# A hybrid decoder layer on one core: transposes at another channel step, LoRA products of a couple's second pair in another turn

## The chip, the cores and the metric

The kernel runs on one core of one Trainium2 chip. The metric is the device time of one execution in microseconds; lower is better. Times before are three runs; one further execution was profiled.

## What is computed

A decoder layer on 2048 rows of 1024 channels in float32: RMS norm, one input projection, two kinds of recurrent heads side by side (four HGRN2 heads of 128 and eight RWKV-7 heads of 64), one output projection, then a gated feed-forward block with a causal convolution, and a last norm. The part that the change touches is the input projection and RWKV's decay and learning rate:

```python
h = _rmsnorm(x, norm1_w[l])
proj = h @ w_in[l]
...
w = -jax.nn.softplus(-(w0 + jnp.tanh(wd) @ w2)) - 0.5      # decay, low-rank ("LoRA")
decay = jnp.exp(-jnp.exp(w))
a = jax.nn.sigmoid(a0 + ad @ a2)                           # learning rate, low-rank
...
kk = heads(k * k_k)
kk = kk / jnp.maximum(jnp.sqrt(jnp.sum(kk * kk, axis=-1, keepdims=True)), L2_EPS)
k = k * (1.0 + (a - 1.0) * k_a)
y = _rwkv7_scan(heads(r), heads(decay), heads(k), heads(v), -kk, kk * heads(a))
```

## The kernel before

The kernel has two stages. The first, up to about 1260 us of the profile, makes the input projection, both kinds of heads and the output projection of the first three blocks of 512 rows; the second makes the rest. Only the first is touched.

The first stage is written as three Python generators whose steps are interleaved by hand. In each round the loop at the stage's end (from L1172 on) lets `rw_super` make one step (a *turn*), then `hg_unit` one, and then calls `fill`, which lets `dense` go on until a budget is used up: `TICK` = 2000 for most rounds, 1.5 or 0.9 times that in some. A channel step of `dense` costs 648 of it, and 436 more where a transpose was issued beside it. So the text puts about three channel steps between two turns.

- `dense` makes the projection column by column: 128 output channels by 512 rows. A column has eight channel steps (`k` = 0 to 7) of three matmuls each (`mm3`, L270 to L272, the high and low parts of the split operands), all into one accumulator in a bank `pj`. After `k` = 7 the column is evicted by ScalarE and VectorE. There are two `pj` banks: one for the column at work, the other for the previous one until it is evicted.
- Beside a column, `dense` issues transposes of rows for later: `turn` (L447, tile `xt`) transposes one 128-channel slice of the next block's normed rows, `turn2` (L457, tile `h`) one of the rows for the second norm, and stores it. Each is four transposes into a `pj` bank and one eviction on ScalarE; `turn2` also sends one store from SP. They lie in the list `turns`; a column takes one at `k` = 1 and, if the list still has one, a second at `k` = 5. There are 24 of the first kind and 16 of the second.
- `rw_super` handles a couple of head pairs: eight RWKV heads are four pairs, a couple is two pairs, so that there are two couples in each of four blocks, eight in all. `U` runs over the couple's pairs. Its matmuls write double banks with the tag `rw`, of which there are two. Its first turn multiplies the LoRA weights `w2a2` with `tl` for both pairs (L722, L723; two products for each pair, one `rw` bank for each pair) and takes the sigmoids `a` and `iW` on ScalarE; its second turn makes a running sum of `iW` on VectorE (`scan`, L731), the squares of the keys and `km` on ScalarE, and splits the squares into high and low parts (`parts`); its third takes exponentials and adds the squares up over a head by matmuls with `group` (L1140, L1141). The last turn of the couple before ends in a product `gm` in an `rw` bank (L991) that VectorE reads at L993.
- `act` loads a table set on ScalarE (L118) whenever a function needs another set than the one before it in the text; sigmoid is in one set, logarithm and exponential are in another. `hg_unit` uses the latter in one of its turns (tile `osq`).

The order of instructions on each engine is fixed when the program is built. It is near that of the text, but not the same: where an instruction's operands or its buffer are judged not to be ready, others that come later in the text go first.

Of the kernel before, what the change touches and what calls it, by code (L numbers as in the profile page):

```python
# [11 lines left out]
AF = mybir.ActivationFunctionType  # L12
ALU = mybir.AluOpType
# [54 lines left out]
def tile_layer(ctx, tc, consts, x, norm1_w, w_in, hg_lb_logits, hg_norm_w, rw_shift_mu, rw_w0, rw_w2,  # L68
# [4 lines left out]
    V, S, TE = nc.vector, nc.scalar, nc.tensor  # L73
# [23 lines left out]
    scanm = cst[:, C_SCAN:C_SCAN + 512]  # L97
# [16 lines left out]
    def act(out_, in_, func, **kw):  # L114

        want = tables.get(func)
        if want is not None and want != tab["now"]:
            pre = S.preload_act_table_set(want)  # L118
            for u_ in tab["uses"]:
                tc.add_manual_dep(pre.ins, u_.ins.name, NOSYNC, reason="table order")  # L120
            tab.update(now=want, pre=pre, uses=[])
        i_ = S.activation(out_, in_, func, **kw)  # L122
        if want is not None:
            tc.add_manual_dep(i_.ins, tab["pre"].ins.name, NOSYNC, reason="table order")
            tab["uses"].append(i_)
        return i_
# [32 lines left out]
    def vec(nm, i):  # L159
        return vt[:, off[nm] + i:off[nm] + i + 1]  # L160
# [20 lines left out]
    oka = cp.tile([P, 16], F32, name="oka")[:, 0:4]  # L181
# [76 lines left out]
    def transposed(xt, nm, psum, evict):  # L258

        n = len(xt)  # L260
        for k in range(KD):
            tp = psum()
            for i in range(n):
                TE.transpose(tp[:, i * P:(i + 1) * P], xt[i][:, k * P:(k + 1) * P], ident)
            evict(k, tp[:, :n * P], vec(nm, k))
            yield 109 * n
# [7 lines left out]
    def phase1(c1):  # L274
# [6 lines left out]
        w2a2 = hp.tile([P, 512], F32, name="w2a2")  # L281
# [156 lines left out]
        def four_tiles(t_):  # L438
            return [t_[:, i, :] for i in range(4)]
# [105 lines left out]
        def spread():  # L545

            while True:
                yield bank("hg")
                yield bank("hg")
                for _ in range(2):  # L550
                    t_ = ps.tile([P, 2, BLK], F32, tag="rw", name="rw", bufs=2)
                    yield t_[:, 0]
                    yield t_[:, 1]

        def dense():
# [49 lines left out]
            def load(i):  # L605
                if i < len(cols) and i not in loaded:
                    ws, ct = [], cols[i] // P
                    for k2 in range(2):
                        if i < NCOL:
                            raw = wp.tile([P, 4, P], F32, tag="wraw", name="wraw", bufs=4)  # L610
                            wload(raw, w_in[0, k2 * 512:k2 * 512 + 512, cols[i]:cols[i] + P].rearrange("(k p) c -> p k c", p=P))
                            ws.append(split(wp, raw, [P, 4, P], "w", 4))
                            for c in range(2):
                                nc.gpsimd.dma_start(Win[ct][k2][c], ws[k2][c].bitcast(F32))
                        else:
                            ws.append(tuple(wp.tile([P, 4, P], F32R, tag="w" + c, name="w" + c, bufs=4) for c in "hl"))
                            for c in range(2):
                                wload(ws[k2][c].bitcast(F32), Win[ct][k2][c])
                    loaded[i] = ws
# [4 lines left out]
            turns = []  # L624
            for n, jb in enumerate(jobs):
                if jb[0] == "E":
                    jb[1]()
                    continue
                if jb[0] == "A":
                    if jb[1] == 0:  # L630
                        banks = spread()
                        ahead = transposed(four_tiles(rows[0]), "n1", lambda: next(banks), to_h)
                    continue
                if jb[0] == "T":
                    turns.append(jb[1])
                    continue
                if jb[0] in "OW":
                    while done["rw2"] < 2 * jb[1] + 2 or done["hg"] < 4 * jb[1] + 4:
                        yield None
                    if jb[0] == "W":  # L640
                        jb[2]()
                    else:
                        yield from (out_block(2, *rows["O"]) if jb[1] == 2 else out_block(jb[1], then=jb[1] + 2, ahead=lambda i=i: load(i)))
                    continue
                if jb[0] == "L":
                    while done["rw1"] < 2 * jb[1] + 4 or done["rw2"] < 2 * jb[1] + 2 or done["hg"] < 4 * jb[1] + 4:
                        yield None
                    (o_half if jb[1] == 2 else o_load)(jb[1])
                    continue
                _, col, ev, cond, fin = jb  # L650
                after = jobs[n + 1][1] if jobs[n + 1][0] == "O" and jobs[n + 1][1] < 2 else None
                while not cond():
                    yield None
                load(i)
                ws = loaded.pop(i)
                if i == 0:
                    next(ahead)
                    next(ahead)
                    constants()
                if jobs[n + 1][0] != "O":  # L660
                    load(i + 1)
                i += 1
                acc = bank("pj")
                then = jobs[n + 1][1] if jobs[n + 1][0] == "A" else None
                for k in range(KD):
                    wh, wl = ws[k // 4]
                    next(ahead, None)
                    mm3(acc, (wh[:, k % 4, :], wl[:, k % 4, :]), (hh[:, k, :], hl[:, k, :]), k == 0, k == KD - 1)
                    aside = k in (1, 5) and len(turns) > 0
                    if aside:  # L670
                        turns.pop(0)()
                    if k == KD - 1:
                        ev(acc)
                        if fin is not None:
                            fin()
                    next_block(then, k)
                    if after is not None:
                        next_out(after, k)
                    yield 648 + 436 * aside
# [18 lines left out]
        U = range(2)  # L698

        def rw_super(nb, s_):  # L700

            tl = stage[("tl", nb)]
            r, k, v = (stage.pop(("rkv", nb, s_, w)) for w in range(3))
            prs = (2 * s_, 2 * s_ + 1)
            pc = [slice(p * P, (p + 1) * P) for p in prs]
# [4 lines left out]
            def bank2():  # L710
                return ps.tile([P, 2, BLK], F32, tag="rw", name="rw", bufs=2)

            def parts(src):
                hi, lo = (rp.tile([P, 2, BLK], F32R, tag=tag, name="part") for tag in ("XH", "E"))
                split_to(hi, lo, src)
                return hi, lo

            ai = tile_("KBT", [2, 2, BLK], "ai")
            a, iW = ai[:, 0], ai[:, 1]
            bs_ = [bank2() for _ in U]  # L720
            for u in U:
                TE.matmul(bs_[u][:, 0, :], w2a2[64:128, pc[u]], tl[64:128, :], start=True, stop=True)  # L722
                TE.matmul(bs_[u][:, 1, :], w2a2[0:64, pc[u]], tl[0:64, :], start=True, stop=True)  # L723
            for u in U:
                act(a[:, u], bs_[u][:, 0, :], AF.Sigmoid, bias=vec("a0", prs[u]))
                act(iW[:, u], bs_[u][:, 1, :], AF.Sigmoid, bias=vec("w0", prs[u]))
            yield
            mk_ = tile_("M", [4, 2, BLK], "mk")
            c, km, sq = mk_[:, 0], mk_[:, 1], mk_[:, 2]
            for u in U:  # L730
                V.tensor_tensor_scan(c[:, u], scanm, iW[:, u], 0.0, ALU.mult, ALU.add)  # L731
                act(sq[:, u], k[:, u], AF.Square, scale=vec("kk", prs[u]))
                act(km[:, u], a[:, u], AF.Identity, bias=oka[:, prs[u]:prs[u] + 1], scale=vec("ka", prs[u]))
            hi, lo = parts(sq)
            yield
            W = tile_("UV", [16, 65], "W")
            WC = tile_("WC", [16, 1], "WC")
# [186 lines left out]
            for u in U:  # L924
                Q, G = M[:, 0, u, :, :, 0:64], M[:, 1, u, :, :, 0:64]
                yg = bank2()
                for w in range(2):
                    for b in range(4):
                        for e in range(2):
                            rs_ = slice(er0(e), er0(e) + 64)  # L930
                            sl = w * 256 + b * 64
                            for h in range(2):
                                rhs = (M[rs_, e, u, b, h, 64:128] if w == 0
                                       else KBT[rs_, u, 2 * b + e, h * 64:h * 64 + 64])
                                TE.matmul(yg[h * 64:h * 64 + 64, e, sl:sl + 64], Q[rs_, b, h, :], rhs,
                                          start=True, stop=True, tile_position=(er0(e), h * 64))
# [8 lines left out]
            for u in U:  # L945
                for ch in range(8):
                    b, e = ch // 2, ch % 2
                    for h in range(2):
# [3 lines left out]
                                  stop=False, tile_position=(0, c0), skip_group_check=True)  # L952
            WC2 = WC.rearrange("p (u c) t -> p u c t", u=2)
            for ch in range(8):
                b, e = ch // 2, ch % 2
                cs_ = slice(ch * 64, ch * 64 + 64)
                for u in U:
                    for h in range(2):
                        hr = slice(h * 64, h * 64 + 64)
                        TE.matmul(xp[hr, u, cs_], M[hr, 1, u, b, e, 0:64], XH[hr, u, ch, :], start=False,  # L960
                                  stop=ch == 7, tile_position=(h * 64, h * 64), skip_group_check=True)
                for u in U:
                    for h in range(2):
                        hr, c0 = slice(h * 64, h * 64 + 64), (h ^ u) * 64
                        TE.matmul(yp[c0:c0 + 64, u, cs_], XH[hr, u, ch, :], RT[hr, u, ch, :], start=False,
                                  stop=ch == 7, tile_position=(h * 64, c0), skip_group_check=True)
# [234 lines left out]
    with ExitStack() as c2:  # L1201
# [36 lines left out]
        with tc.tile_pool(name="op", bufs=1, reuse_waits="tile") as op_:  # L1238
# [61 lines left out]
            for dh in range(2):  # L1300
                accs = [pst("wacc") for _ in range(4)]
                for n, k in enumerate((0, 1, 4, 5, 2, 3, 6, 7)):
# [22 lines left out]
                    for q in range(12):  # L1325
                        i, t_ = (q % 4, q // 4) if first else (q // 3, q % 3)
                        TE.matmul(accs[i], terms[t_][0][:, i * P:(i + 1) * P], terms[t_][1],
                                  start=n == 0 and t_ == 0, stop=n == KD - 1 and t_ == 2)
# [353 lines left out]
```

## Time and profile before

| | us |
|---|---|
| three runs | 2602.02, 2597.45, 2592.02; median 2597.45 |
| profiled execution | 2593.87 |
| its span, first to last instruction | 2592.1 |
| PE busy | 2526.2 (97%) |
| VectorE (DVE) busy | 1961.6 (76%) |
| ScalarE (ACT) busy | 1381.2 (53%) |
| GpSimd (POOL) busy | 371.4 (14%) |

PE is TensorE's matmuls, PEld its weight loads, which overlap them. A group's row names the line, the engine, the operation, the tiles written and read, the shape and the count, then busy time and mean length of one, then the engine's idle time before them and what ended it. In the timeline a row is start, length, engine, line, operation, tiles and count; a bracket at its end is the idle time before it and who ended it. A matmul's end is modelled: where matmuls overlap, their rate is read from the distance of the starts.

### The profile page before, as it was taken

How to read it: one execution, taken by the hardware profiler on the slowest of the kernel's cores; microseconds unless marked ns; L12 is line 12 of the kernel's file. 1: busy time of each engine (PE TensorE's matmuls, PEld its weight loads, DVE VectorE, ACT ScalarE, POOL GpSimd, SP SyncE). 2: the span in 40 equal slices, each digit the busy share in tenths (PEclk: the TensorE clock that was granted, in tenths of full speed). 3: DMA queues.
4: the chain of work that ended last, by engine and by line, in shares of the span. 5: the costliest groups of instructions: out<-in, count | busy, mean ns of one | idle time of the engine just before them, and what ended most of it. 6: DMA issues, size and time to landing. Idle time of an engine off the chain costs nothing.

```text
span 2592.1 us, 50957 instructions
## 1 busy us (share of the span) xinstructions
PE 2526.2 (97%) x19467; PEld 2034.7 (78%) x19467; DVE 1961.6 (76%) x3744; ACT 1381.2 (53%) x2266; POOL 371.4 (14%) x660
## 2 busy tenths in 40 slices
PE   7999999999999999999999999999999999999998
PEld 6777778777777777777788888877888878888887
DVE  4878777685666866788687799988988887666555
ACT  5556554564445644355567644565555454455444
POOL 6433222222222122231000000000000000000000
PEclk9999999999999999999999999999999999999999
DMA  8846455575745657676663477757653564988655
GB/s 310 240 156 192 154 161 146 156 207 176 210 156 159 196 176 196 237 222 171 234 206 126 141 258 252 231 178 232 215 196 101 180 200 134 330 313 289 195 187 191
DMA packets 379722, 518.98 MB, mean 200 GB/s; under 512 B 113887, under 2 KB 210517, under 8 KB 379477
## 3 DMA queue, kind: packets, MB, share of 16 engines
q1 hardware_dynamic: 325361, 337.38, 41.0%
q0 software_dynamic: 54048, 178.32, 21.5%
q8 instruction: 153, 2.51, 0.4%
q14 instruction: 92, 0.75, 0.1%
q10 hardware_dynamic: 68, 0.02, 0.0%
HBM read 372.99 MB, written 134.22 MB: 196 GB/s over the span
## 4 chain that ended last, share of the span: by engine, by line
PE 58%; issue 14%; DVE 12%; DMA 6%; ACT 5%; POOL 4%; SPq 0%; POOLq 0%; DVEq 0%; ACTq 0%
PE pj L270 6%; PE pj L271 5%; PE pj L272 5%; PE ua L270 4%; PE ua L272 4%; PE ua L271 4%; PE da L270 3%; PE da L271 3%; PE da L272 3%; PE db L271 2%; PE db L272 2%; PE db L270 2%; PE ud L272 2%; PE ud L270 2%; PE ud L271 2%
## 5 line engine op out<-in xcount | busy, mean ns | idle before, releaser
L270 PE MATMUL pj<-hh,wh 128*128 128x512 f32 x960 | 394.6, 411 | 1.3 <-ACT xt L122 0.9
L271 PE MATMUL pj<-hl,wh 128*128 128x512 f32 x960 | 378.3, 394 | 0.0
L272 PE MATMUL pj<-hh,wl 128*128 128x512 f32 x960 | 378.0, 394 | 0.0
L270 PE MATMUL ua<-Bh,uwh 128*128 128x512 f32 x704 | 277.0, 393 | 4.0 <-ACT m L122 3.7
L272 PE MATMUL ua<-Bh,uwl 128*128 128x512 f32 x704 | 274.5, 390 | 1.9 <-DVE uwl L255 1.9
L271 PE MATMUL ua<-Bl,uwh 128*128 128x512 f32 x704 | 274.2, 389 | 0.0
L270 PEld LDWEIGHTS pj<-hh,wh 128*128 128x128 f32 x960 | 180.9, 189 | 47.0 <-issue 4.9
L272 PEld LDWEIGHTS pj<-hh,wl 128*128 128x128 f32 x960 | 180.9, 188 | 40.4 <-issue 1.2
L271 PEld LDWEIGHTS pj<-hl,wh 128*128 128x128 f32 x960 | 181.2, 189 | 36.2 <-issue 3.2
L254 ACT CAST uwh<-uraw 128x512 fp32r<-128x512 f32 x220 | 134.5, 617 | 132.6 <-PE ua L271 53.5
L255 DVE TENSOR_TENSOR dal<-draw,dah 128x512 fp32r<-128x512 f32 x138 | 95.2, 690 | 110.9 <-ACT dah L254 110.5
L254 ACT CAST dah<-draw 128x512 fp32r<-128x512 f32 x138 | 85.8, 622 | 164.2 <-PE da L271 77.3
L255 DVE TENSOR_TENSOR uwl<-uraw,uwh 128x512 fp32r<-128x512 f32 x220 | 147.0, 684 | 34.6 <-ACT uwh L254 34.4
L270 PEld LDWEIGHTS ua<-Bh,uwh 128*128 128x128 f32 x704 | 132.1, 188 | 35.9 <-ACT m L122 8.9
L272 PEld LDWEIGHTS ua<-Bh,uwl 128*128 128x128 f32 x704 | 132.2, 188 | 30.5 <-DVE uwl L255 2.8
L271 PEld LDWEIGHTS ua<-Bl,uwh 128*128 128x128 f32 x704 | 132.2, 188 | 26.7
L270 PE MATMUL ud<-Bh,uwh 128*128 128x512 f32 x352 | 138.0, 392 | 0.0
L272 PE MATMUL ud<-Bh,uwl 128*128 128x512 f32 x352 | 137.1, 390 | 0.0
L271 PE MATMUL ud<-Bl,uwh 128*128 128x512 f32 x352 | 137.0, 389 | 0.0
L1552 POOL DMA_DIRECT2D gd<-y x2 | 1.1, 541 | 945.9 <-DVE y L1550 945.9
L271 PE MATMUL da<-dbl,dah 128*128 128x512 f32 x332 | 129.5, 390 | 0.2 <-DVE dbl L255 0.2
L272 PE MATMUL da<-dbh,dal 128*128 128x512 f32 x332 | 129.2, 389 | 0.0
(589 smaller groups left out, 6181.1 us busy)
## 6 DMA issues: line engine op xcount, KB each, us to landing
uraw<-in_w_up_dram SPq DMA_DIRECT2D x176, 256.0 KB, 3.2
br<-gd SPq DMA_DIRECT2D x88, 256.0 KB, 4.2
draw<-Sg SPq DMA_DIRECT2D x88, 256.0 KB, 2.8
draw<-Tw SPq DMA_DIRECT2D x88, 256.0 KB, 3.8
gd<-y SPq DMA_DIRECT2D x86, 256.0 KB, 2.8
Sg<-br SPq DMA_DIRECT2D x72, 256.0 KB, 2.2
xt<-x1d SPq DMA_DIRECT2D x32, 512.0 KB, 6.6
wraw<-in_w_in_dram POOLq DMA_DIRECT2D x60, 256.0 KB, 4.8
```

Of the source, the lines that this page charges most:

```text
L254: S.copy(hi, src)
L255: V.tensor_sub(lo, src, hi.bitcast(F32))
L270: TE.matmul(acc, lh, rh, start=first, stop=False, skip_group_check=skip)
L271: TE.matmul(acc, lh, rl, start=False, stop=False, skip_group_check=skip)
L272: TE.matmul(acc, ll, rh, start=False, stop=last, skip_group_check=skip)
L1552: (dma if end is None else nc.gpsimd.dma_start)(gd_[2 * h + b][fb * P:(fb + 1) * P, :], ys[0][:, b * BLK:(b + 1) * BLK])
```

## The change

Two edits in the first stage. A column's first transpose stands at channel step 2 instead of 1. In `rw_super` the LoRA products and sigmoids of the couple's second pair go from the first turn to the second, where the running sums and `km` of both pairs follow; the squares of the keys and their split go from the second turn to the first. The number of turns is the same, and no instruction is added or removed in the text.

```diff
-                    aside = k in (1, 5) and len(turns) > 0
+                    aside = k in (2, 5) and len(turns) > 0
...
-            bs_ = [bank2() for _ in U]
-            for u in U:
-                TE.matmul(bs_[u][:, 0, :], w2a2[64:128, pc[u]], tl[64:128, :], start=True, stop=True)
-                TE.matmul(bs_[u][:, 1, :], w2a2[0:64, pc[u]], tl[0:64, :], start=True, stop=True)
-            for u in U:
-                act(a[:, u], bs_[u][:, 0, :], AF.Sigmoid, bias=vec("a0", prs[u]))
-                act(iW[:, u], bs_[u][:, 1, :], AF.Sigmoid, bias=vec("w0", prs[u]))
-            yield
             mk_ = tile_("M", [4, 2, BLK], "mk")
             c, km, sq = mk_[:, 0], mk_[:, 1], mk_[:, 2]
+
+            def lora(u):
+                b_ = bank2()
+                TE.matmul(b_[:, 0, :], w2a2[64:128, pc[u]], tl[64:128, :], start=True, stop=True)
+                TE.matmul(b_[:, 1, :], w2a2[0:64, pc[u]], tl[0:64, :], start=True, stop=True)
+                act(a[:, u], b_[:, 0, :], AF.Sigmoid, bias=vec("a0", prs[u]))
+                act(iW[:, u], b_[:, 1, :], AF.Sigmoid, bias=vec("w0", prs[u]))
+
+            def scan(u):
+                V.tensor_tensor_scan(c[:, u], scanm, iW[:, u], 0.0, ALU.mult, ALU.add)
+                act(km[:, u], a[:, u], AF.Identity, bias=oka[:, prs[u]:prs[u] + 1], scale=vec("ka", prs[u]))
+
+            lora(0)
             for u in U:
-                V.tensor_tensor_scan(c[:, u], scanm, iW[:, u], 0.0, ALU.mult, ALU.add)
                 act(sq[:, u], k[:, u], AF.Square, scale=vec("kk", prs[u]))
-                act(km[:, u], a[:, u], AF.Identity, bias=oka[:, prs[u]:prs[u] + 1], scale=vec("ka", prs[u]))
             hi, lo = parts(sq)
+            yield
+            lora(1)
+            for u in U:
+                scan(u)
             yield
```

## Prediction

> **What bounds the kernel now.** I read the busy table first, then stages, then PE's groups with their idle time, then the timeline around the two edited places.
>
> ```profile
> span 2592.1 us, 50957 instructions
> PE 2526.2 (97%) x19467; PEld 2034.7 (78%) x19467; DVE 1961.6 (76%) x3744; ACT 1381.2 (53%) x2266; POOL 371.4 (14%) x660
> ...
> 50.00:1240.00 1190.00, 1156.80 (x13437) 912.10 (x13436) 869.15 (x2075) 635.29 (x1054) 322.12 (x572) 1.00 0.62 186
> 1240.00:2592.10 1352.10, 1333.82 (x5880) 1094.41 (x5878) 1068.96 (x1614) 720.32 (x1163) 16.43 (x30) 1.00 0.63 209
> ```
>
> PE is the bound: busy 97% of the span, at granted clock 1.00 in both stages. All edited code runs in the first stage. From 50 to 1240 us PE is idle 1190.0 - 1156.8 = 33.2 us, spread over 1.2 ms; no edit here removes PE work, so only a part of those 33 us can be won. The groups name the part that touches the edit:
>
> ```profile
> L270 PE MATMUL pj<-hh,wh 128*128 128x512 f32 x960 | 394.6, 411 | 1.3 <-ACT xt L122 0.9 <-DVE hq L346 0.2
> L1140 PE MATMUL rw<-part,group 128*128 128x512 f32 x48 | 19.7, 410 | 1.3 <-ACT part L247 1.3
> L1141 PE MATMUL rw<-part,group 128*128 128x512 f32 x48 | 19.3, 401 | 0.4 <-DVE part L248 0.4
> L722 PE MATMUL rw<-tl,w2a 64*128 64x512 f32 x32 | 17.4, 633 | 3.7 <-DVE yo L993 2.5 <-ACT ai L122 1.2
> L447 PE MATMUL pj<-ident,xt 128*128 128x128 f32 x96 | 15.1, 279 | 4.4 <-DVE hgg L370 2.0 <-DVE hq L346 1.4 <-ACT hf L122 0.9
> L457 PE MATMUL pj<-ident,xt 128*128 128x128 f32 x64 | 9.9, 275 | 0.7 <-ACT h L122 0.4 <-DVE hq L346 0.4
> ```
>
> These are groups of PE's instructions: busy us, mean ns of one, then the idle time before them and what ended it. The LoRA products (L722) wait 3.7 us. The transposes of the next block's rows (L447) wait 4.4 us, those of the second norm (L457) 0.7: 5.1. The head sums (L1140, L1141) wait 1.7. Everything that the edit names is 10.5 us, 0.4% of the span.
>
> **How far the order on the engines is that of the text.** A couple's timeline on PE:
>
> ```profile
> 485.69 0.69 PE L722 MATMUL rw<-tl,w2a 64*128 64x512 f32 x1
> ...
> 488.01 0.39 PE L272 MATMUL pj<-hh,wl 128*128 128x512 f32 x1
> 488.25 0.40 PE L270 MATMUL pj<-hh,wh 128*128 128x512 f32 x1
> 489.41 0.69 PE L722 MATMUL rw<-tl,w2a 64*128 64x512 f32 x1 [0.77 <-ACT ai L122]
> ...
> 490.47 0.50 PE L271 MATMUL pj<-hl,wh 128*128 128x512 f32 x1
> ...
> 492.43 0.40 PE L1140 MATMUL rw<-part,group 128*128 128x512 f32 x1
> ```
>
> The text issues a couple's four products in one go (each shows as two instructions), but on PE the second head pair's two start 3.7 us after the first, with dense matmuls between. So the builder had judged the second `rw` bank not yet free and had put ready matmuls ahead; it only guessed 0.77 us too short. Matmuls follow each other every 0.23 us (488.01 to 488.25), so a channel step of three is 0.69 us, though a single one shows 0.39. The head sums, two turns behind, come 8 dense matmuls later (490.47 to 492.43): a turn is about 9 dense matmuls, 2.1 us, and other heads' work.
>
> **Part 1, the second pair a turn later.** How many `pj` matmuls already lie between the pairs of the six couples that wait, by the table of stretches for that tile (length, then PE's busy us and its count in brackets), and below them the waits from the timeline:
>
> ```profile
> 204.79:207.90 3.11, 2.57 (x10) 1.78 (x10) 0.17 (x1) 0.60 (x1) 1.00 0.01 3
> 348.75:351.20 2.45, 2.11 (x8) 1.41 (x8) 0.00 (x0) 0.09 (x1) 1.00 0.00 0
> 486.76:489.40 2.64, 1.88 (x7) 1.22 (x7) 0.00 (x0) 0.60 (x1) 1.00 0.38 135
> 658.96:660.80 1.84, 1.17 (x5) 0.75 (x5) 0.00 (x0) 0.00 (x0) 1.00 0.86 324
> 799.55:802.20 2.65, 2.11 (x8) 1.41 (x8) 0.03 (x1) 0.60 (x1) 1.00 0.65 198
> 1121.14:1123.30 2.16, 1.08 (x4) 0.75 (x4) 0.00 (x0) 0.00 (x0) 1.00 0.55 197
> ```
>
> ```profile
> 351.28 0.69 PE L722 MATMUL rw<-tl,w2a 64*128 64x512 f32 x1 [0.42 <-ACT ai L122]
> 660.84 0.69 PE L722 MATMUL rw<-tl,w2a 64*128 64x512 f32 x1 [0.72 <-DVE yo L993]
> 802.24 0.66 PE L722 MATMUL rw<-tl,w2a 64*128 64x512 f32 x1 [0.58 <-DVE yo L993]
> 1123.35 0.69 PE L722 MATMUL rw<-tl,w2a 64*128 64x512 f32 x1 [0.58 <-DVE yo L993]
> ```
>
> A turn later means at least 9 between. The cover grows by 0, 1, 2, 4, 1 and 5 matmuls of 0.23 us. The waits are 0.42, 0.77, 0.72, 0.58 and 0.58 as quoted, and 3.7 less these, 0.6, in the first. What is left of them: 0.6, 0.19, 0.31, 0, 0.35, 0, in sum 1.45. Gain: 3.7 - 1.45 = 2.2 us. Ends: 0 (the builder puts the pair where it stands) and 3.7 (all gone). I take 2.2, because the row count says the move is only some 2 matmuls on average. Behind the waiting pair on PE stand only dense matmuls; nobody else waits for it. In the other two couples (60.87 and 981.94) the second pair never waited, so a turn's delay of 2.1 us gains nothing; it makes the second scan later there, and dense matmuls cover that, as between 485.69 and 489.41. The pair's sigmoids go along on ACT, the second `scan` and `km` follow on DVE and ACT in the turn in which they stood before. No DMA moves with this part, and neither SP's nor POOL's queue is passed.
>
> **Part 2, squares a turn sooner.** In the trace they are long done:
>
> ```profile
> 475.66 0.71 ACT L122 ACTIVATE mk<-rkv,vt 128x512 f32<-128x512 f32 x1
> ...
> 479.52 1.05 ACT L247 CAST part<-mk 128x1024 fp32r<-128x1024 f32 x1 [1.59 <-PE rw L1140]
> ```
>
> Square at 475.66, cast done at 480.57, 5.1 us before the first product at 485.69 and 12 us before the sums that read it (492.43). A turn sooner in the text changes nothing that PE sees: 0. Ends: -1.7 us (the head sums' waits, were they these sums') and +0.7 (the two squares a place too early on ACT, 0.71 ahead of an eviction).
>
> **Part 3, transposes at step 2.** A transpose at step 1 must find the bank that the previous column's accumulator held. The dense matmuls from a column's first up to its transposes, by the same kind of table, for the three longest waits, and the waits:
>
> ```profile
> 239.57:243.00 3.43, 1.51 (x7) 0.93 (x5) 0.68 (x1) 0.59 (x1) 1.00 0.88 185
> 497.89:503.00 5.11, 3.63 (x15) 2.36 (x13) 0.72 (x1) 0.60 (x1) 1.00 0.73 210
> 824.26:827.00 2.74, 1.53 (x7) 0.93 (x5) 0.70 (x1) 0.60 (x1) 1.00 0.45 124
> ```
>
> ```profile
> 243.02 0.66 PE L447 MATMUL pj<-ident,xt 128*128 128x128 f32 x4 [1.39 <-DVE hq L346]
> 503.07 0.66 PE L447 MATMUL pj<-ident,xt 128*128 128x128 f32 x4 [1.36 <-DVE hgg L370]
> 827.06 0.65 PE L447 MATMUL pj<-ident,xt 128*128 128x128 f32 x4 [0.62 <-DVE hgg L370]
> ```
>
> Of each count one is the previous column's last. So at 243.02 and 827.06 the transposes stand at 6 matmuls, where the text puts them; at 503.07 at 14, already later than step 2 (9), and the move does nothing there. Three matmuls more cover 0.69 of the 1.39 and all of the 0.62: 1.3 us gained. The smaller waits I count at nothing. Ends: 0 and 5.1. I take 1.3, by these rows. What goes along: four transposes, the eviction on ACT (`xt`, 0.60; `h`, 0.69) and, for eight of the second kind, a store on SP, 0.69 us later and past no other transfer that waits for it. What comes late next is the bank: the tile of step 2 must be out three steps, 9 x 0.23 = 2.07 us, later for a second tile at step 5, instead of four. That I cost at nothing; it is the third rival.
>
> **Sum.** 2.2 + 0 + 1.3 = 3.5 us off the span, 2592.1 to 2588.6. The profiled execution took 2593.87 us with 1.8 around the span, so 2590.4. The three runs' median, 2597.45, lies 3.6 above the profiled one; on its scale the forecast is 2594.0. That is 0.13%, under the 0.5% (13 us) that a measurement here tells from no change.
>
> **Rivals.**
>
> *It doesn't do what it says* (15%): the builder fills PE by its own guess of readiness, as the 7 matmuls ahead of 489.41 show, and ends with the same order. 2597.5. Against it: at 243.02 and 827.06 the text's place was kept.
>
> *All the named waits go* (15%): 10.5 us, 2587 on the median's scale. For it: none of the waits is over 1.4 us, about one turn. Against it: the 1.36 at 503.07 stands at 14 matmuls, where a later step in the text does not reach. A redrawn order of the whole first stage might carry it further; its entire idle time is 33.2 us, and under 2584 some 40% of that would have to go.
>
> *Slower: the second tile waits for the bank* (13%). Eight columns carry two tiles. If an eviction ends over 2.07 us after its transposes start, the next transposes stop PE, and behind them the column.
>
> ```profile
> 984.66 0.60 PE L457 MATMUL pj<-ident,xt 128*128 128x128 f32 x4
> ...
> 986.12 0.70 ACT L122 ACTIVATE h<-pj,vt 128x512 f32<-128x512 f32 x1
> ```
>
> Here it ended 2.16 us after (986.82 - 984.66), longer than the three steps that will be left. If all eight lose the whole step, 8 x 0.69 = 5.5 us; with part 1's gain and without part 3's, 2597.45 - 2.2 + 5.5 = 2600.8. It decides against the change once more than five of the eight lose a step (5 x 0.69 = 3.5).
>
> *Slower: tables* (7%). Sigmoids in two turns instead of one can have a head's logarithm and exponential between them, and each such couple needs two more table loads.
>
> ```profile
> L118 ACT ACT_TABLE_LOAD x50 | 64.2, 1283 | 0.9
> ...
> 1124.53 1.26 ACT L122 ACTIVATE ai<-rw,vt 128x512 f32<-128x512 f32 x2 [1.32 <-PE rw L723]
> 1125.81 1.28 ACT L118 ACT_TABLE_LOAD   x1
> 1127.11 0.69 ACT L122 ACTIVATE osq<-hg,eps 128x512 f32<-128x512 f32 x1
> ```
>
> For it: in the last couple a head's logarithm (1127.11) already stands right behind the sigmoids. Price: at most 16 loads of 1.283, 20.5 us of ACT, which is idle half the stage. If all of it showed, 2594.0 + 20.5 = 2614.5; if one couple has it and it shows, 2594.0 + 2.6 = 2596.6. [...]
>
> **How the numbers follow.** Part of the waits goes: 50%, 2594.0. The rivals hold 15, 15, 13 and 7%. The range reaches down past 2587 by the spread of the runs (2592.02 to 2602.02, about 5 either way) to 2581, and up past the bank's 2600.8 by some 3 to 2604; without the far ends of the last two rivals some two in ten lie outside. The likeliest case alone has 2589 to 2599. Faster by over 0.5% needs the tail of the second rival, 6%; slower by over 0.5% the full price of the tables or both slow rivals, 5%; the rest, 89%, is within.
>
> **What would show it.** L722's idle time falls from 3.7 to about 1.5 and L447's and L457's together from 5.1 to about 3.8; the second pair stands 9 or more dense matmuls behind the first; squares still end before the products; the table loads between 50 and 1262 us stay near 50; the second stage stays at its time. The prediction is wrong if the first stage's PE idle time moves by more than 10 us, which would be a redrawn order and not the named waits, or if `h` or `xt` appears as a releaser of the dense matmuls with more than today's 0.9.

## Result and the profile after

The changed kernel took 2606.3 us (median of 16 executions, 2599.3 to 2614.2) against 2597.9 for the kernel before (16, 2590.8 to 2602.9): ratio 1.0027, 95% interval 1.0016 to 1.0037. By the medians it is 8.4 us slower, some 0.3%; the forecast was 3.5 us faster, and its range ended at 2604. In two later comparisons the same kernel had 1.0031 (1.0019 to 1.0044) and 1.0020 (1.0010 to 1.0030).

The profiled execution of the changed kernel happens to be its slowest (2614.17) and that of the kernel before a quick one (2593.87). So the two profiles lie 20 us apart where the medians lie 8.4 apart: kinds and places are read from them, sizes from the timed ratios.

The busy table of the changed kernel:

```profile
span 2612.2 us, 50948 instructions
...
PE 2537.7 (97%) x19467; PEld 2044.8 (78%) x19467; DVE 1963.4 (75%) x3744; ACT 1382.9 (53%) x2266; POOL 371.0 (14%) x660
```

Its two stages by the table of stretches (length, then busy us and instructions of PE, PEld, DVE, ACT and POOL, then granted clock, DMA share, GB/s):

```profile
50.00:1240.00 1190.00, 1151.28 (x13181) 906.83 (x13183) 858.85 (x2046) 627.42 (x1039) 322.88 (x574) 0.99 0.60 183
1240.00:2612.20 1372.20, 1353.42 (x6151) 1111.97 (x6151) 1081.57 (x1643) 730.89 (x1179) 17.85 (x32) 1.00 0.63 209
```

The second stage kept its length: from its first matmul on the tile `ua` to the end it takes 1287.5 us before and 1289.2, 1286.9 and 1285.3 in the three profiles of the changed kernel (`after_again` and `after_again2` are the other two). So the loss lies in the first, where PE has done 13181 matmuls by 1240 us instead of 13437. Two things took time there: PE idles 1190.0 - 1151.3 = 38.7 us instead of 33.2, and its clock was granted at half rate for 23.9 us of the stage instead of 10.2 (added up from the clock records). The clock's column has to be read closely: a mean that reads 1.00 or 0.99 still holds 10 or 24 us at half rate.

PE's groups, those that the prediction named and those that grew (line numbers behind the edit are 3 or 7 higher than before: L722 is L725, L1140 is L1147, L960 is L967, L886 is L893; in the kernels below with a line `late` they are 3 or 11 higher):

```profile
L270 PE MATMUL pj<-hh,wh 128*128 128x512 f32 x960 | 397.9, 415 | 1.4 <-ACT xt L122 0.6 <-ACT hv L122 0.5
L270 PE MATMUL pj<-wh,hh 128*128 128x512 f32 x160 | 66.3, 420 | 8.4 <-DVE hgg L370 5.4 <-DVE xh L417 2.7
L271 PE MATMUL pj<-wl,hh 128*128 128x512 f32 x160 | 63.8, 399 | 2.2 <-DVE wl L255 2.2
L967 PE MATMUL rw<-XH,M 64*64 64x64 f32 x512 | 29.2, 231 | 1.7 <-DVE XH L974 1.7
L1147 PE MATMUL rw<-part,group 128*128 128x512 f32 x48 | 20.0, 417 | 3.6 <-ACT part L247 3.6
L725 PE MATMUL rw<-tl,w2a 64*128 64x512 f32 x32 | 18.0, 642 | 1.8 <-ACT ai L122 1.6
L447 PE MATMUL pj<-ident,xt 128*128 128x128 f32 x96 | 15.0, 280 | 0.8 <-DVE hq L346 0.8
L457 PE MATMUL pj<-ident,xt 128*128 128x128 f32 x64 | 9.8, 275 | 0.1
L893 PE MATMUL rw<-TTs,ZT 32*32 32x32 f32 x512 | 7.9, 195 | 2.9 <-ACT ZT L122 2.6
```

Before, the groups of these that the prediction did not show were:

```profile
L270 PE MATMUL pj<-wh,hh 128*128 128x512 f32 x160 | 66.1, 420 | 7.3 <-DVE hgg L370 5.4 <-DVE xh L417 1.7
L271 PE MATMUL pj<-wl,hh 128*128 128x512 f32 x160 | 64.1, 401 | 0.0
L960 PE MATMUL rw<-XH,M 64*64 64x64 f32 x512 | 29.5, 230 | 0.1
L886 PE MATMUL rw<-TTs,ZT 32*32 32x32 f32 x512 | 7.6, 194 | 1.8 <-ACT ZT L122 1.7
```

The edit did what it was read to do, and more: the LoRA products' idle time fell from 3.7 to 1.8 us, the transposes' from 5.1 to 0.9. These 6.1 us, and more, came back elsewhere: the head sums (L1147) rose from 1.3 to 3.6, the product on `XH` from 0.1 to 1.7, the output projection from 7.3 to 8.4 behind `xh` and from 0 to 2.2 behind its weights `wl`, the products on `ZT` from 1.8 to 2.9, in sum 8.3 us. The rest of the 5.5 us more is spread over groups that rose by 1 us or less each.

### The profile page after: what moved, and what is told of

It is laid out like the page before. It is cut to its first block, busy times and chain, and to the rows that moved or that the text cites. A ratio compares the mean times of both kernels' runs of the same rounds, so it can differ in the third digit from the quotient of the medians.

```text
span 2612.2 us, 50948 instructions
## 1 busy us (share of the span) xinstructions
PE 2537.7 (97%) x19467; PEld 2044.8 (78%) x19467; DVE 1963.4 (75%) x3744; ACT 1382.9 (53%) x2266; POOL 371.0 (14%) x660
## 4 chain that ended last, share of the span: by engine, by line
PE 61%; issue 13%; DVE 11%; DMA 7%; ACT 4%; POOL 3%; SPq 0%; POOLq 0%; DVEq 0%; ACTq 0%
PE pj L270 5%; PE pj L271 5%; PE pj L272 5%; PE ua L270 5%; PE ua L272 5%; PE ua L271 5%; PE da L271 3%; PE da L272 3%; PE da L270 3%; PE ud L272 2%; PE ud L270 2%; PE ud L271 2%; PE db L270 2%; PE db L272 2%; PE db L271 2%
```

## The experiments

Each ratio is against the kernel before on the same chip, with its 95% interval. The kernel before had medians of 2597.7, 2595.0, 2596.7 and 2597.2 us beside the four sets. The ratio is not the quotient of the medians and differs from it by up to 0.001.

**First set: which half of the change.** `turns_only` is the kernel before with the transposes' edit; `rw_only` with all of the edit in `rw_super` and the transposes at step 1; `squares_only` with the squares a turn sooner and both LoRA pairs in the first turn; `after_again` is the changed kernel.

```diff
turns_only, against before:
-                    aside = k in (1, 5) and len(turns) > 0
+                    aside = k in (2, 5) and len(turns) > 0
squares_only, against before:
-            yield
             mk_ = tile_("M", [4, 2, BLK], "mk")
             c, km, sq = mk_[:, 0], mk_[:, 1], mk_[:, 2]
             for u in U:
-                V.tensor_tensor_scan(c[:, u], ...)
                 act(sq[:, u], ...)
-                act(km[:, u], ...)
             hi, lo = parts(sq)
             yield
+            for u in U:
+                V.tensor_tensor_scan(c[:, u], ...)
+                act(km[:, u], ...)
+            yield
```

> Only the transposes go to step 2; the LoRA products stay in the first turn. Theory CHAIN (the loss comes from the LoRA edit, which makes a couple's chain on ACT and DVE later, so that PE waits at its head sums): 2594 to 2598, that is 0 to 4 us under before, with L447 and L457 idle under 1.5 us together. Rival BANK (a step less for the second transposes): 2602 to 2606, with xt or h as releasers of dense matmuls. Rival CLOCK (short PE stops cluster and trip half-clock windows, whichever edit causes them): the time follows the number of windows at half clock, about 1.7 us for each 3.4 us.

> Only the LoRA and squares edit; transposes stay at step 1. Theory CHAIN: 2603 to 2608, all or more of the loss, with the head sums' idle time near 4 us as in the changed kernel and BV's cast about 1.5 us later in the first couple. Rival BANK: 2594 to 2598. Rival CLOCK: in between, and more than two half-clock windows.

> Only the squares go a turn sooner; the LoRA products of both pairs stay in the first turn. Built, the order on every engine is that of the kernel before, so all theories expect no change, 2594 to 2602, and the profile is a second one of the kernel before: CHAIN and BANK expect its stops at the same places within 0.3 us; CLOCK expects that the number and place of half-clock windows may differ.

> The changed kernel once more, for a second profile on the same chip as the parts. CHAIN: 2602 to 2610, head sums idle again near 4 us. CLOCK: 2602 to 2610, and half-clock windows again more than two before 1260 us; where the first profile's windows were luck, the count falls to two or three and the profiled time with it by about 1.7 us for each.

| kernel | us | ratio to before | interval |
|---|---|---|---|
| turns_only | 2596.8 | 1.0002 | 0.9988 to 1.0016 |
| rw_only | 2600.6 | 1.0020 | 1.0011 to 1.0029 |
| squares_only | 2595.4 | 0.9997 | 0.9985 to 1.0008 |
| after_again | 2603.7 | 1.0031 | 1.0019 to 1.0044 |

The squares do nothing that these runs can tell. The transposes alone neither gain nor lose, so the bank of the second tile costs nothing by itself; they keep 3.2 us of their waits, where CHAIN expected under 1.5. The LoRA edit alone loses. By the medians it loses less than the whole change (2600.6 against 2603.7) and less than the 2603 that CHAIN expected at least, though the two intervals overlap. Against CLOCK: the profile of `turns_only` has 20.5 us at half clock in the first stage, as `after_again` has, and took 2593.5 us, as long as that of the kernel before with 10.2. So the time at half clock alone does not give the loss.

**Second set: which couples.** In these the second pair is a turn later only in some of the eight couples, numbered 0 to 7 (squares as in the changed kernel; where the pair is not later, its products follow the first pair's sigmoids in the text):

```diff
+            late = 2 * nb + s_ in (1, 2, 3, 4, 5)
             lora(0)
+            if not late:
+                lora(1)
             for u in U:
...
             yield
-            lora(1)
+            if late:
+                lora(1)
             for u in U:
                 scan(u)
```

`lora_1to5` has the couples 1 to 5 as shown, `lora_06` has 0 and 6, `lora_7` the last, all with the transposes at step 1; `lora_1to5_turns` is `lora_1to5` with the transposes at step 2.

> Second pair a turn later in the last couple alone; transposes at step 1. Theory TABLES IN THE LAST COUPLE (its second sigmoids stand behind a head's logarithm, exponential and two table loads; the second scan is 3 us later; a half-clock window follows near 1208 us): 2600 to 2603, the whole loss of rw_only. Rival NO-WAIT COUPLES (the loss comes from the first and seventh couples, where the second pair never waited): 2596 to 2598. Rival SCATTER (no couple carries it): 2597 to 2600.

> Second pair a turn later in the first and the seventh couple alone, where it never waited before; transposes at step 1. TABLES IN THE LAST COUPLE: 2596 to 2598. NO-WAIT COUPLES: 2600 to 2603, with the first couple's BV cast 1.5 us later and more idle time at the head sums and at the products behind them. SCATTER: 2597 to 2600.

> Second pair a turn later in the second to sixth couples, where it waited 3.1 us in all before; transposes at step 1. TABLES IN THE LAST COUPLE and NO-WAIT COUPLES: 2595 to 2597.5, some 1 to 2 us of the LoRA waits gone and nothing lost. SCATTER: 2598 to 2600.

> As lora_1to5, with the transposes at step 2. If the two edits do not touch each other: 2594 to 2597, below the kernel before. If they do (the transposes' stop in the fourth couple is gone and PE comes 1.8 us early to the head sums, then waits at XH and xh and meets half-clock windows near 510, 588 and 773 us as in the changed kernel): 2599 to 2602.

| kernel | us | ratio to before | interval |
|---|---|---|---|
| lora_7 | 2597.0 | 1.0011 | 1.0000 to 1.0021 |
| lora_06 | 2595.2 | 0.9999 | 0.9991 to 1.0008 |
| lora_1to5 | 2595.7 | 1.0001 | 0.9993 to 1.0010 |
| lora_1to5_turns | 2599.1 | 1.0020 | 1.0009 to 1.0032 |

Two places lose: the last couple by itself, and something in the couples 1 to 5 that neither edit makes alone (1.0002 and 1.0001) but both together do. The first is only just seen in the times: the interval of `lora_7` begins at 1.0000, and its 2597.0 us lie under the 2600 to 2603 that were expected. The traces show it more clearly.

*The last couple.* ACT's timeline in the changed kernel:

```profile
1135.71 1.27 ACT L122 ACTIVATE ai<-rw,vt 128x512 f32<-128x512 f32 x2 [0.53 <-PE rw L726]
1136.99 1.28 ACT L118 ACT_TABLE_LOAD   x1
1138.29 0.69 ACT L122 ACTIVATE osq<-hg,eps 128x512 f32<-128x512 f32 x1
...
1139.58 0.62 ACT L122 ACTIVATE osq<-osq 128x512 f32<-128x512 f32 x1
1140.22 1.28 ACT L118 ACT_TABLE_LOAD   x1
1141.51 1.26 ACT L122 ACTIVATE ai<-rw,vt 128x512 f32<-128x512 f32 x2
```

Before, the second pair's sigmoids (1124.53) followed the first pair's by 3.3 us:

```profile
1121.24 1.27 ACT L122 ACTIVATE ai<-rw,vt 128x512 f32<-128x512 f32 x2 [0.53 <-PE rw L723]
```

Now it is 5.8: the head's logarithm and exponential, with a load on either side, have moved between the pairs. How long a couple takes is read from its first LoRA product to its last product `gm` (both by their lines' list of instructions, count, shortest/median/longest, first and last start), here for the last couple before and after:

```profile
L722 PE MATMUL rw<-tl,w2a x4: 589/641/694, 1120.1 to 1123.9; 64*128 64x512 f32 x4
L991 PE MATMUL rw<-gdt,g x8: 590/592/630, 1116.2 to 1247.9; 128*128 128x512 f32 x8
```

```profile
L725 PE MATMUL rw<-tl,w2a x4: 589/642/694, 1134.5 to 1138.4; 64*128 64x512 f32 x4
L998 PE MATMUL rw<-gdt,g x8: 590/592/647, 1130.6 to 1265.9; 128*128 128x512 f32 x8
```

127.8 us (1247.9 - 1120.1) has become 131.4. Over all 18 profiled executions of this case, read in the same way, the last couple takes 130.5 to 131.9 us in the seven where its second pair is later and 127.4 to 128.6 in the eleven where it is not.

*The clock.* The table of stretches, for the changed kernel, cut so that each pair is the 3.41 us before a stretch at half clock and that stretch:

```profile
506.99:510.40 3.41, 1.64 (x8) 0.94 (x7) 3.41 (x5) 2.48 (x4) 0.73 (x2) 0.99 0.87 315
510.40:513.81 3.41, 3.41 (x11) 2.79 (x10) 3.21 (x4) 0.60 (x1) 0.00 (x0) 0.51 0.65 223
...
1216.89:1220.30 3.41, 2.13 (x80) 1.33 (x76) 3.32 (x10) 3.05 (x7) 0.00 (x0) 1.00 0.49 175
1220.30:1227.13 6.83, 6.72 (x69) 5.33 (x70) 6.18 (x17) 2.79 (x7) 2.15 (x4) 0.50 0.51 155
```

PE was idle for 52% and 38% of the stretch before, and the next ran at 0.5. With the last couple's pair later PE comes to `ZT` and `TTs` ahead of ACT, some 85 us behind the couple's start: in `lora_7` PE is idle there for 53% of 3.41 us, and the half clock follows.

```profile
1203.49:1206.90 3.41, 1.60 (x67) 1.05 (x66) 3.35 (x10) 3.12 (x8) 0.54 (x1) 0.99 0.36 125
1206.90:1210.31 3.41, 3.41 (x51) 2.84 (x53) 3.41 (x9) 0.81 (x3) 1.61 (x3) 0.51 0.57 192
```

A half-clock stretch that starts between 1206 and 1221 us is in all seven profiles with the last couple's pair later and in none of the eleven others. In the changed kernel dense matmuls start 0.42 us apart inside a half-clock stretch (511.31 to 511.73) and 0.23 outside (514.06 to 514.29), so a stretch costs at most about half its length, here 1.7 or 3.4 us; this is an estimate.

**Third set: where the two edits meet.** In the traces of `turns_only` and `lora_1to5_turns` the fourth couple (3) starts at nearly the same time, its first LoRA product at 489.62 and 489.28 us. The fifth starts at 662.27 and 666.71, so the fourth takes 172.7 us in one and 177.4 in the other, 4.8 more. Its stop near 507 us, in `turns_only`, then in `lora_1to5_turns`:

```profile
506.89 0.33 PE L447 MATMUL pj<-ident,xt 128*128 128x128 f32 x1 [1.28 <-DVE hgg L370]
```

```profile
506.60 0.50 PE L1151 MATMUL rw<-part,group 128*128 128x512 f32 x1 [1.77 <-ACT part L247]
...
624.81 0.39 PE L971 MATMUL rw<-XH,M 64*64 64x64 f32 x6 [2.58 <-DVE XH L978]
```

The stop at the transposes is gone, but the head sums stop at the same time. Behind it PE comes to the product on `XH` 2.6 us before VectorE has made it; a stretch of 3.41 us at half clock follows at 625.5 (1.7 us lost, by the same estimate). 2.6 + 1.7 = 4.3 is most of the 4.8. What VectorE is doing, in the changed kernel, with ACT's rows that it waits for:

```profile
622.19 0.07 DVE L745 MEMSET W<- 128x16 f32 x1
627.01 0.75 DVE L435 TENSOR_SCALAR xt<-xt,nst 128x1024 f32<-128x1024 f32 x1 [4.75 <-ACT nst L122]
627.68 0.28 DVE L974 TENSOR_TENSOR XH<-rw,WC 128x128 f32<-128x128 f32 x1
```

```profile
616.51 1.06 ACT L122 ACTIVATE nsq<-xt 128x1024 bf16<-128x1024 f32 x1 [6.01 <-DMA xt<-x1d]
...
623.43 1.06 ACT L122 ACTIVATE nsq<-xt 128x1024 bf16<-128x1024 f32 x1 [1.27 <-DMA xt<-x1d]
...
625.11 1.28 ACT L118 ACT_TABLE_LOAD   x1
```

`XH` stands on VectorE behind the norm (L435) of the first block's rows, which come back from DRAM (`x1d`) for the second norm. That waits 4.75 us for ACT's factors, these for a table load, that for the last square, and that for a transfer. A chain that has nothing to do with the couple holds its `XH`. In the kernel before, `XH` stands behind the same norm, but PE has no wait for it there:

```profile
615.51 0.75 DVE L435 TENSOR_SCALAR xt<-xt,nst 128x1024 f32<-128x1024 f32 x1 [2.67 <-ACT nst L122]
616.18 0.28 DVE L967 TENSOR_TENSOR XH<-rw,WC 128x128 f32<-128x128 f32 x1
```

Four kernels test the place:

```diff
c3_turns, not3_turns, after_no7: as in the second set, transposes at step 2, with
+            late = 2 * nb + s_ in (3,)
+            late = 2 * nb + s_ in (1, 2, 4, 5)
+            late = 2 * nb + s_ in (0, 1, 2, 3, 4, 5, 6)
after_n_later, against the changed kernel:
-                              (at[nb] + 7, ("E", norm4(("N", nb - 2))))]
-                    extra += [(at[nb] + 8 + k // 2, ("T", turn2(...
+                              (at[nb] + 7 + 2 * (nb == 2), ("E", norm4(("N", nb - 2))))]
+                    extra += [(at[nb] + 8 + 2 * (nb == 2) + k // 2, ("T", turn2(...
```

> The second pair later in the fourth couple alone, transposes at steps 2 and 5. FOURTH COUPLE: here the turn's delay lets TensorE run on past the two stops near 493 and 507 us that the transposes alone had, so that it comes to the product on XH (L971) before VectorE has done the norm of the rows that came back from DRAM; a wait of 1.5 to 3 us at XH near 625 us, a stretch of half clock behind it in some executions, and a ratio of 1.0015 to 1.002 as with the couples 1 to 5. ANYWHERE: what the two edits do to each other is spread over the couples or is mere scatter: 1.000 to 1.0005 and no wait over 0.9 us at XH.

> The second pair later in the couples 1, 2, 4 and 5, not in the fourth (3), transposes at steps 2 and 5. FOURTH COUPLE: no wait over 0.9 us at XH, the stop near 507 us stays, ratio 0.9995 to 1.0005. ANYWHERE: 1.001 to 1.002, as with the couples 1 to 5.

> The changed kernel, but in the last couple the second pair stays with the first. ADDITIVE: the last couple's tables are worth 0.0011, so that this comes to 1.0015 to 1.002 against the kernel before, the half-clock stretch near 1220 us is gone, and the last couple is some 3 us shorter than in the changed kernel. ONE CAUSE: all of the loss comes from the tables, and this comes to 1.000; or all of it comes from the fourth couple, and this stays at 1.003.

> The changed kernel, but the norm of the first rows that come back from DRAM, and their transposes, are put two columns later (some 12 us each), so that the norm no longer stands ahead of the product XH of the fourth couple on VectorE. NORM IN THE WAY: the wait at XH near 628 us (1.7 us) goes, VectorE's own wait for the rows' factors goes down from some 4 or 5 us to under 1, and the ratio falls from 1.003 to 1.001 or 1.002, if no later stop takes its place. NOT THE NORM: XH still waits for more than 1 us there, and the ratio stays at 1.003.

| kernel | us | ratio to before | interval | stop near 507 us | wait at XH |
|---|---|---|---|---|---|
| c3_turns | 2598.9 | 1.0011 | 0.9998 to 1.0024 | head sums 1.76 | 1.64 |
| not3_turns | 2596.8 | 1.0000 | 0.9990 to 1.0011 | transposes 1.27 | 0.84 |
| after_no7 | 2601.1 | 1.0014 | 1.0002 to 1.0025 | head sums 1.74 | 0.99 |
| after_n_later | 2599.3 | 1.0006 | 0.9995 to 1.0017 | head sums 1.77 | none |

`not3_turns` loses nothing. `c3_turns` shows both stops of the fourth couple with that couple alone later, but its ratio is half of that of `lora_1to5_turns`, under the expected 1.0015, and its interval goes down to 0.9998. `after_no7` comes to 1.0014, close to what ADDITIVE expected: its last couple takes 127.5 us and has no half clock behind it. With the norm moved, to 671 us, `XH` is free and VectorE no longer waits ahead of the norm, but the head sums still stop. The two groups of `after_n_later`:

```profile
L967 PE MATMUL rw<-XH,M 64*64 64x64 f32 x512 | 29.2, 230 | 0.0
L1147 PE MATMUL rw<-part,group 128*128 128x512 f32 x48 | 19.8, 413 | 3.9 <-ACT part L247 3.8
```

The ratio, 1.0006, fell further than the expected 1.001, and by more than the wait, so the move had to be tried on its own.

**Fourth set: controls and both remedies.** `before_n_later` is the kernel before with only that move of the norm; `after_n_later2` and `after_again2` repeat two kernels side by side; `no7_n_later` is the changed kernel with the move and with the last couple's pair left in the first turn (both edits shown above).

> The kernel before, with only the norm of the first rows that come back from DRAM, and their transposes, two columns later. NORM IN THE WAY: the kernel before has no wait at XH there, so nothing is gained: 0.9995 to 1.0005. GOOD ANYWHERE: the move helps whatever the kernel, 0.998 or less.

> The changed kernel with the norm two columns later, again, beside the changed kernel on one chip. NORM IN THE WAY: 1.0005 to 1.0015, 0.0015 to 0.0025 under the changed kernel. SCATTER: no more than 0.0005 under it.

> The changed kernel once more: 1.0025 to 1.0035 by every theory; it is here as the neighbour of the others of this call.

> The changed kernel with the last couple's second pair left where it was and the norm two columns later. Both parts of the loss mended (tables of the last couple 0.0011, norm in the fourth): 0.9995 to 1.0005. If something else takes part: 1.001 or more.

| kernel | us | ratio to before | interval |
|---|---|---|---|
| before_n_later | 2596.0 | 0.9994 | 0.9983 to 1.0005 |
| after_n_later2 | 2599.3 | 1.0010 | 0.9999 to 1.0021 |
| after_again2 | 2602.4 | 1.0020 | 1.0010 to 1.0030 |
| no7_n_later | 2597.7 | 1.0002 | 0.9992 to 1.0012 |

On one chip the moved norm takes 0.0010 (3.1 us by the medians) off the changed kernel, less than the expected 0.0015 to 0.0025, and in the kernel before 0.0006 with an interval that holds 1. These intervals overlap, so the times do not show that the move is worth more where `XH` waits. The changed kernel itself, at 1.0020, came out under the 1.0025 that was expected of it at least.

The traces separate the kernels better. The length of the fourth couple, from its first LoRA product to that of the fifth, over the 18 profiles:

| kernels | profiles | length of the fourth couple, us |
|---|---|---|
| kernel before and all others that have not both edits in the fourth couple | 9 | 171.8 to 173.8 |
| both edits there, the norm in its place (`after` 177.3) | 6 | 174.7 to 178.7 |
| both edits there, the norm two columns later | 3 | 172.4, 172.4 and 174.0 |

So both edits together make this couple 2 to 7 us longer, and with the norm moved most of that is gone; in the kernel before the move changes it by 0.4 (172.2 to 171.8). With both remedies no loss is left that these runs can tell: 1.0002 in `no7_n_later` against 1.0020 in the changed kernel beside it, and the two intervals do not meet. The first stage of `no7_n_later`:

```profile
50.00:1240.00 1190.00, 1156.67 (x13412) 909.99 (x13413) 868.56 (x2072) 632.95 (x1051) 325.96 (x574) 1.00 0.61 186
```

Its groups:

```profile
L971 PE MATMUL rw<-XH,M 64*64 64x64 f32 x512 | 29.2, 230 | 0.1
L1151 PE MATMUL rw<-part,group 128*128 128x512 f32 x48 | 19.8, 413 | 3.5 <-ACT part L247 3.4
L725 PE MATMUL rw<-tl,w2a 64*128 64x512 f32 x32 | 18.0, 641 | 2.0 <-ACT ai L122 1.3 <-DVE yo L1004 0.6
L447 PE MATMUL pj<-ident,xt 128*128 128x128 f32 x96 | 14.8, 276 | 0.9 <-DVE hq L346 0.8
L457 PE MATMUL pj<-ident,xt 128*128 128x128 f32 x64 | 9.9, 276 | 0.5 <-ACT hf L122 0.4
```

The transposes' and LoRA products' waits are nearly as short as in the changed kernel (3.4 us together against 2.7), PE's idle time is 33.3 us, as before the change (33.2), and the time is the same as before. None of the versions beats the kernel before by what these measurements can tell.

What stays open: the profile of `after_again2` shows no wait at `XH`, and yet its fourth couple takes 174.7 us and the kernel has 1.0020. So that wait differs between executions (1.7 us in `after`, none here; ahead of it ACT waits for transfers of the rows, in `after` 6.01, 0.85 and 1.27 us), and it is not all of the loss there; a half-clock stretch at 508 us, behind the stop at the head sums, is another part. The move of the norm also shifts other work. Why the rows land some 5 us later against the couple than in the kernel before (the last square starts 131.7 us behind the couple's first LoRA product in `after`, 126.3 before) was not tried. Between the two places (0.0011 and 0.0010 in their own comparisons) and the whole (0.0020 to 0.0031) up to 0.001 is left that no single kernel pinned, and `rw_only` lost 0.0020 on one chip where the LoRA edit's three parts add up to 0.0011 on another; stretches at half clock (five in the first stage of the changed kernel's profile, two before) and the wait for `wl`, which is 0.1 us in `no7_n_later`, may be in it, and were not tried by themselves. Against `wl` speaks `turns_only`, which waits 2.4 us there and loses nothing.

## Why the prediction failed

- **Part 1, size of the wait: right.** 3.7 was to fall to about 1.5 and fell to 1.8.
- **Part 2: right.** `squares_only` is at 0.9997, and its order on the engines is that of the kernel before.
- **Part 3: about right alone, too small together.** With the transposes alone their waits fell by 1.9 us, not far from the 1.3; in the changed kernel they fell by 4.2. That the move does nothing at 503.07 holds with the transposes alone (1.28 remains there) but not with the LoRA pair a turn later, which redraws the order around it.
- **The step that failed is the sum.** It takes the removed waits off the span at face value and costs what is late next at nothing; only the bank and the tables are named, as rivals. The waits were really gained, 6.1 us of them, and bought nothing: 8.3 us of waits came up at other places, the last couple became 3.6 us longer and the fourth 5.1 (172.2 to 177.3). `turns_only`, too, removed 1.9 us of transposes' waits (5.1 to 3.2) at a ratio of 1.0002, with PE idle for 33.6 us of the first stage as against 33.2. In the fourth couple the stop only moved: from the transposes at 503 us to the head sums at 509 and to `XH` at 628. Our reading is that, where PE already issues whatever is ready, the wait removed in front of one reader was the slack that the next reader lived on.
- **"Dense matmuls cover that"** was said of the two couples that never waited, where it held (`lora_06` 0.9999). Of the last couple it was taken as well, unsaid, and there it failed: its chain became 3.6 us longer, and some 85 us on PE waited at `ZT` and `TTs`.
- **The rival of the tables had the place right and the chance wrong.** It named the last couple and the logarithm behind the sigmoids, and priced one couple at 2.6 us; `lora_7` lost 0.0011, 2.9 us. Its mechanism differed: no load was added (49 from 50 to 1262 us, 50 before, and 61 in all in both). The second pair's sigmoids wait behind two loads of 1.28 us that were there anyway. It had 7%, though the row quoted for it already showed the order that decides.
- **The rival of the bank is refuted.** `turns_only` loses nothing, and in the changed kernel `xt` releases the dense matmuls for 0.6 us, less than the 0.9 before.
- **The clock was not in it.** "Granted clock 1.00 in both stages" is a rounded mean; stretches of half clock were there before and grew from 10.2 to 23.9 us in the first stage of the profiles. Half of the 13.7 us more is 6.8 us, an estimate of what that cost the slow profile.
- **The signs of failure** were PE's idle time moving by 10 us, or `h` or `xt` as a releaser. Neither came: it moved by 5.5. The sign to name would have been a wait that appears in a group which had none, as `XH` did.

## What to carry to other kernels

Here, with one engine 97% busy and its order packed by readiness, 6.1 us of removed waits gained nothing and 8.3 us came up elsewhere, so a wait's removal is not to be counted before the chain behind it is seen to be ready sooner; ask of each removed stop which reader of the same chain comes next, and look up whether its input is any earlier. A step moved by a turn is to be followed in every repetition of the loop, the last one too. In the last couple the place of the table loads in ACT's order decided, not their number (49 from 50 to 1262 us against 50). When two harmless edits lose together, the place is found by halving over the repetitions and over the stretches of the trace.

## What was unexpected of the hardware

The clock fell to half behind far less than a full stop. The 18 profiles have 54 half-clock stretches in the first stage behind its start; in the 3.41 us ahead of each PE was idle for about 25% or more, and in 49 of them for over 35%, often split over several waits. In the seven of `before` and `after` it was 38 to 72%; ahead of the stretch at 1220.30 it was 1.3 us of 3.41 (1216.89). The same idle share does not always have a half clock behind it. Before the change PE was idle for 40% of these 3.41 us, and no half clock followed:

```profile
499.66:503.07 3.41, 2.05 (x9) 1.32 (x8) 3.41 (x6) 3.22 (x4) 1.07 (x2) 1.00 0.80 247
```

In the first stage of these two profiles the stretches are 3.41 or 6.83 us long, one length or two, and in each trace their starts lie whole multiples of that length apart too (745.87 - 510.35 = 235.52 us = 69 x 3.413 in the changed kernel; 37 lengths from 735.39 to 861.69 before). The distances do not explain, though, why the same idle share is followed by a half clock in one place and not in another: the row above starts 0.2 us off a whole number of lengths from its trace's stretches (69 ahead of 735.39), and in these 3.41 us of the changed kernel, 34 lengths behind 510.35, PE is idle for 1.62 us and no half clock follows:

```profile
626.40:629.81 3.41, 1.79 (x26) 1.62 (x26) 2.80 (x7) 1.84 (x9) 0.35 (x1) 1.00 0.44 154
```

Why a half clock follows in one case and not in the other stays open.
